# Two-layer pooling and HGRN2 trunk: one 128x128 product for a block's attention weights, and 32 bytes of padding among the activations

## The chip, the core and the metric

The kernel runs on one core of a Trainium2 chip. Its engines run side by side, each through its own list of instructions, and meet through semaphores: TensorE multiplies (PE in the profile; its weight loads are listed apart as PEld), VectorE (DVE) and ScalarE (ACT) read TensorE's results from PSUM and work in SBUF, GpSimd (POOL) works in SBUF, SyncE (SP) issues most transfers. The metric is the device time in microseconds (us), lower being better, as the median of several runs.

## What is computed

The input is 512 tokens of 1024 channels, float32. Layer 0 is a pooling mixer, layer 1 an HGRN2 mixer; each has a projection in, the mixer on 2048 inner channels, a gate, a projection out and a residual sum, and a final RMSNorm closes the trunk. The change lies in layer 1 (and in where the activations of both layers lie). For each of its 16 heads of 128 channels:

```python
log_f = logaddexp(log(lb), log1p(-lb) + log_sigmoid(fz))       # forget gate, per channel
k = (1 - lb) * sigmoid(-fz)
# o_t = S_t^T q_t  with  S_t = diag(f_t) S_{t-1} + k_t v_t^T
A[t, s] = sum_d q[t, d] * k[s, d] * exp(b[t, d] - b[s, d])      # s <= t, b = cumulative log_f
o = A @ v + (q * exp(b)) @ S
o = o * rsqrt(mean(o * o) + eps) * norm_g
y = (o * silu(gate)) @ w_out
```

## The kernel before

Activations lie channel-major ([channel, token]) in SBUF. The large projections multiply float32 numbers as three one-pass products of exact halves (`mm3`, L125 to L128: hi by hi, lo by hi, hi by lo), each with 128x128 weights loaded and 512 columns streamed past them. The streamed halves of the layer's input are xh0 to xh7 and xl0 to xl7 (`scaled_halves`, L197, in the pool `act`); those of the pooled values are ph and pl, of a mixer's result zh and zl (layer 0), z1h and z1l, and zz for the last group (layer 1, 256 columns a time). Weights arrive in pieces of 512 KB (`piece`, L97): SyncE issues the transfer into wraw, ScalarE casts the high half whi (L94), VectorE subtracts for wlo (L95).

Layer 1 goes through its heads in four groups of four (`group`, L425). For a group, `prepare` makes gates, keys and queries, `inputs` the values (here the pieces of the weights are streamed and slices of xh and xl are loaded as weights), and then `heads` (L576) does, on TensorE without large products between:

- `within` (L542) for each of the four heads: the weights of its four blocks of 128 tokens as plain float32 products, which TensorE runs in two passes each. A block takes two products that load 64 columns each: L549 (keys of the first half, 128 queries) into PSUM partitions 0 to 63, L550 (keys of the second half, only the 64 queries that can see them) into partitions 64 to 127. Then three transposes of the keys (L556). VectorE copies the causal part into Ad (L552, L553), ScalarE the transposed keys into kt (L558).
- `state` (L561) for each head: three products kt by vn (L567), which VectorE turns into the carried states st (L573, L574).

`attend` (L580) later multiplies Ad and the states with values and queries (L587, L589).

All these results go to the PSUM pool `pa` with four buffers. A product can only start when the buffer that it gets has been read: a head's transposes or weights wait for the copies of a head before it, and the second head's `state` product waits for the copy L553 of the third head. The large products have a pool `ps` of their own. The order on every engine is fixed when the program is built.

A second, general form of layer 1 (`levels`) lies behind a condition that is not met with these inputs; it doesn't run.

Of the kernel before, what the change touches and what calls it, by code (L numbers as in the profile page):

```python
"""Two-layer streaming-encoder trunk: multi-scale causal pooling mixer, then HGRN2, on one core.

Activations are kept channel-major ([channel, token]), so every projection contracts over
partitions.  float32 products with long moving operands run as three one-pass float32r products of
exact halves (x = hi + lo, 12 significant bits each): hi*hi + hi*lo + lo*hi.  Short ones run as
plain float32 products.

The RMSNorm factor of a token commutes with the projection, so it is applied where the projection's
result leaves PSUM.

HGRN2 is computed as causal linear attention.  The decay between tokens s < t is the product of the
forget gates of s+1..t.

Factored form: within a block of 128 tokens the decay is a ratio of products taken to the block's middle,
one factor going to k and one to q; from block to block the state is carried.  The products over half a
block must not run out of range for this; whether they did is recorded on the way.

General form, for any gates, run over the layer when the record says so: a pair is served at the one
level h (1, 2, 4, ..) at which s and t lie in sibling blocks of h tokens; the decay is then (s to the end
of its block) * (start of t's block to t), both at most one, so nothing can overflow.  The running products  # L20
are lengthened from level to level by the sibling's total.
"""
# [10 lines left out]
F32 = mybir.dt.float32  # L33
# [5 lines left out]
PSUM = bass.MemoryType.PSUM  # L39
# [5 lines left out]
KD = D // P          # 8 channel tiles of the model width  # L45
KI = DI // P         # 16 channel tiles of the inner width
NG = 4               # groups of the inner width
GC = DI // NG        # 512 channels a group
GT = GC // P         # 4 channel tiles a group
TB = T // P          # 4 token blocks  # L50
# [4 lines left out]
NORM_AT, SPREAD_AT = (KD - 2, 2), (KD - 1, 1)   # where in its first projection (step, tile)  # L55
AHEAD = 300           # how far, in traced instructions, the weights run ahead of their use
FLOOR = 1e-26         # the least product of gates over half a block that the factored form takes
LEVELS = (1, 2, 4, 8, 16, 32, 64)

# columns of the packed parameters  # L60
# [5 lines left out]
def trunk(ctx: ExitStack, tc: tile.TileContext, xT, par, ident_d, causal_d, mask_d, w0_in, w0_grp, w0_out, w1_in, w1_out, outT):  # L66
# [9 lines left out]
    # ---- parameters and constants  # L76
    ones = const.tile([P, P], F32, name="ones")
    nc.gpsimd.memset(ones, 1.0)
    # the tensor engine's clock comes up, and the function table in, while the first loads are on their way
# [17 lines left out]
    def piece(src):  # L97
        """A [128, 2, 512] piece of a weight as exact halves."""
        raw = wpool.tile([P, 2, GC], F32, name="wraw", tag="wraw", bufs=RAW)
        hi = wpool.tile([P, 2, GC], F32R, name="whi", tag="whi", bufs=WB)  # L100
        lo = wpool.tile([P, 2, GC], F32R, name="wlo", tag="wlo", bufs=WB)
        with tc.high_priority(AHEAD):
            nc.sync.dma_start(out=raw, in_=src)
            split(raw, hi, lo)
        return hi, lo

    def load_in(w, col=0):
        """512 columns of a projection: one pair of halves a row tile."""
        v = w.rearrange("(k p) n -> p k n", p=P)
        out = []  # L110
        for i in range(v.shape[1] // 2):
            hi, lo = piece(v[:, 2 * i:2 * i + 2, col:col + GC])
            out += [(hi[:, 0], lo[:, 0]), (hi[:, 1], lo[:, 1])]
        return out

    def load_out(w, g):
        """Rows of group g of a [2048, 1024] projection, one row tile a piece."""
        out = []
        for i in range(GT):
            r = g * GC + i * P  # L120
            hi, lo = piece(w[r:r + P, :].rearrange("p (a b) -> p a b", a=2))
            out.append((hi.rearrange("p a b -> p (a b)"), lo.rearrange("p a b -> p (a b)")))
        return out
# [6 lines left out]
    def project4(pieces, xs, norm):  # L130
        """The four channel tiles of 512 columns, advancing together through the contraction.  The norm's
        short products go in before the end, so that its result is there in time."""
        accs = [ps.tile([P, T], F32, name="mm", tag="mm", bufs=4) for _ in range(GT)]
        for k, ((wh, wl), (xh, xl)) in enumerate(zip(pieces, xs)):
            for n, acc in enumerate(accs):
                if (k, n) == NORM_AT:
                    rn = norm()
                if (k, n) == SPREAD_AT:
                    rb = spread_sbuf(rn)
                c = slice(n * P, (n + 1) * P)  # L140
                mm3(acc, wh[:, c], wl[:, c], xh, xl, k == 0, k == len(pieces) - 1)
        return accs, rn, rb

    def project(pieces, n, xs):
        """[128 channels, 512 tokens] of a projection: columns n*128.. of the pieces."""
        acc = ps.tile([P, T], F32, name="mm", tag="mm", bufs=4)
        c = slice(n * P, (n + 1) * P)
        for k, ((wh, wl), (xh, xl)) in enumerate(zip(pieces, xs)):
            mm3(acc, wh[:, c], wl[:, c], xh, xl, k == 0, k == len(pieces) - 1)
        return acc  # L150

    def rms(name, srcs, cols=slice(0, T)):
        """1/rms of each token over the channel tiles, [token, block]."""
# [29 lines left out]
    def spread(rn):  # L183
        """[token, block] -> [any channel, token], in PSUM."""
# [11 lines left out]

    def scaled_halves(k, col):  # L197
        g = pp[:, col + k:col + k + 1]
        hi = act.tile([P, T], F32R, name=f"xh{k}", tag=f"xh{k}", bufs=1)
        lo = act.tile([P, T], F32R, name=f"xl{k}", tag=f"xl{k}", bufs=1)  # L200
        nc.scalar.activation(out=hi, in_=h[k], func=AF.Copy, scale=g)
# [14 lines left out]
    # ---- layer 0: pooling mixer  # L216
# [83 lines left out]
    # kept for the general form of the next layer  # L300
# [4 lines left out]
    # ---- layer 1: HGRN2 mixer  # L305
    # lower bounds of this layer: softmax over the layers, cumulated, less the first
# [14 lines left out]
    def hgrn(ctx, general):  # L321
# [4 lines left out]
        # attention weights within a token block: zeroed once, later only the causal part is written  # L326
# [67 lines left out]
        def normed(o, so):  # L394
            """Each token of a head divided by its rms; so is left with the sums of squares."""
# [13 lines left out]
        def gated(g, n, on, gate, last):  # L409
            """Back to [channel, token], times the norm's weight and the gate."""  # L410
# [14 lines left out]
        def group(g, prepare, heads, zs):  # L425
            """One group of heads: the rest of its projections, its heads, and the output products of the
            group before, which keep the tensor engine busy meanwhile."""
# [19 lines left out]
        def finish(zs):  # L447
            """Last output product and final norm, one half of the tokens after the other."""
# [11 lines left out]
            def scaled(half, i, bc, rb):  # L460
                """Two channel tiles of the result; the first two by way of the engines that are free."""
# [27 lines left out]
        def factored():  # L489
            """Decays within a block of 128 tokens as ratios to its middle; between blocks by the state.  # L490
            Returns how many of the marks that say that the ratios stayed in range are set."""
# [9 lines left out]
            def store(f, pr, j, hd, s1):  # L501
                """In a block's first half at t the gate of t + 1 (one in the middle), in the second that of t."""
# [7 lines left out]
            def prepare(g):  # L510
# [3 lines left out]
                for pr in range(2):  # L514
# [6 lines left out]
                    # products over the halves, the first with the block's first gate as well  # L521
# [20 lines left out]
            def within(n):  # L542
                """Weights within the blocks; the tokens after the middle do not weigh on those before."""
# [3 lines left out]
                for b in range(TB):  # L547
                    c, m = b * P, b * P + 64
                    nc.tensor.matmul(a[0:64, b], k[:, c:m], q[:, c:c + P], start=True, stop=True)  # L549
                    nc.tensor.matmul(a[64:P, b, 64:P], k[:, m:c + P], q[:, m:c + P], start=True, stop=True)  # L550
# [10 lines left out]
            def state(g, n, kt, v):  # L561
                """The state that each block but the first starts from, taken on to the block's middle; by way
                of the block's start, as the two factors' product may be out of range."""
# [35 lines left out]
            # in range: no product over half a block under the floor, and every sum of squares finite  # L599
# [12 lines left out]
        def levels():  # L612
# [16 lines left out]
            def self_weights(pr, f, kk, q):  # L629
                """A token with itself: the decay is one.  Then q takes its own gate."""  # L630
# [8 lines left out]
            def level(pr, li, hh, tot, kk, q, off):  # L639
                """Pairs of sibling blocks of hh tokens; then the products are lengthened to 2 hh."""  # L640
# [90 lines left out]
def _masks():  # L731
    """For each level, which (s, t) of a token block lie in sibling blocks, for the t's in odd blocks."""
# [40 lines left out]
```

## Time and profile before

| what | value |
|---|---|
| device time, three runs | 845.63, 845.29, 845.55 us; median 845.55 us |
| span of the profiled execution, first to last instruction | 844.7 us |
| TensorE busy | 829.0 us, 98% of the span, 4134 passes |
| VectorE busy | 550.5 us, 65% |
| ScalarE busy | 274.6 us, 33% |
| GpSimd busy | 171.7 us, 20% |
| mean granted TensorE clock | 0.992 |
| HBM traffic | 92 GB/s over the span |

The profile's page gives the span of the profiled execution and no time of its own beside it; 845.55 less 844.7 leaves 0.85 us around the span. Starts are counted from the span's start. A matmul's duration in a row runs from its start to a modelled end, and the next one starts before that; the distance from start to start is what a product costs, and the texts below go by starts. A merged row (x24) stands for so many passes that follow one another.

### The profile page before, as it was taken

What the parts mean: (1) busy time and instruction counts of PE and PEld (TensorE: products, weight loads), DVE (VectorE), ACT (ScalarE), POOL (GpSimd) and SP (SyncE); (2) the same over time, 40 slices, a digit from 0 to 9 for tenths busy, and PEclk for the clock granted to TensorE, in tenths of its full rate; (3) what the DMA queues carried; (4) which work ended last, traced back from release to release, by engine and by line L of the source; (5) the groups of instructions that cost most, each with busy time, mean ns of one, the idle gap of its engine ahead of it and who ended that gap; (6) DMA issues with size and microseconds to landing.
All of it is one profiled execution on the core that took longest, in us unless ns stands there. A gap on an engine that the chain in (4) does not pass through costs nothing.

```text
span 844.7 us, 10684 instructions
## 1 busy us (share of the span) xinstructions
PE 829.0 (98%) x4134; PEld 691.7 (82%) x4134; DVE 550.5 (65%) x845; ACT 274.6 (33%) x472; POOL 171.7 (20%) x218
## 2 busy tenths in 40 slices
PE   9899999999999999999999999999999999999995
PEld 7688888888888888888888888888888888888895
DVE  7766645754685465799269963279963279963643
ACT  7352224213333144323332232332332332334231
POOL 5020001001002023170314300315300305203024
PEclk9999999999999999999999999999999999999997
DMA  6622333123423145133033331233331133320203
GB/s 217 209 70 84 99 100 100 55 96 100 150 99 100 54 163 180 57 95 105 1 100 100 100 100 30 71 100 100 99 101 39 62 100 100 100 100 1 74 2 104
DMA packets 37931, 78.56 MB, mean 93 GB/s; under 512 B 2800, under 2 KB 5104, under 8 KB 37872
## 3 DMA queue, kind: packets, MB, share of 16 engines
q1 hardware_dynamic: 35744, 74.98, 27.9%
q10 hardware_dynamic: 2128, 2.81, 0.9%
q8 instruction: 34, 0.56, 0.3%
q14 instruction: 25, 0.20, 0.1%
HBM read 73.59 MB, written 4.19 MB: 92 GB/s over the span
## 4 chain that ended last, share of the span: by engine, by line
PE 91%; DVE 4%; DMA 2%; POOL 1%; issue 1%; ACT 1%; SPq 0%; ACTq 0%; DVEq 0%; POOLq 0%
PE mm L126 28%; PE mm L128 27%; PE mm L127 27%; PE a L587 2%; DVE wlo L95 1%; PE a L549 1%; PE a L589 1%; PE a L567 1%; DVE r L534 1%; DMA wraw<-in_w0i 1%; PE a L414 1%; PE a L556 1%; DMA h<-in_xT 0%; DMA wraw<-in_w1i 0%; PE a L188 0%
## 5 line engine op out<-in xcount | busy, mean ns | idle before, releaser
L126 PE MATMUL mm<-xh,whi 128*128 128x512 f32 x640 | 251.3, 393 | 0.9 <-DVE v L242 0.4
L128 PE MATMUL mm<-xh,wlo 128*128 128x512 f32 x640 | 249.8, 391 | 1.6 <-DVE wlo L95 1.6
L127 PE MATMUL mm<-xl,whi 128*128 128x512 f32 x640 | 249.6, 390 | 0.0
L94 ACT CAST whi<-wraw 128x1024 fp32r<-128x1024 f32 (+1 forms) x140 | 141.8, 1025 | 249.8 <-PE mm L127 168.9
L95 DVE TENSOR_TENSOR wlo<-wraw,whi 128x1024 fp32r<-128x1024 f32 (+1 forms) x140 | 173.4, 1265 | 58.2 <-ACT whi L94 57.2
L128 PEld LDWEIGHTS mm<-xh,wlo 128*128 128x128 f32 x640 | 120.4, 188 | 28.6 <-DVE wlo L95 3.2
L126 PEld LDWEIGHTS mm<-xh,whi 128*128 128x128 f32 x640 | 120.6, 188 | 26.6 <-ACT whi L94 1.1
L127 PEld LDWEIGHTS mm<-xl,whi 128*128 128x128 f32 x640 | 120.5, 188 | 24.5
L214 DVE TENSOR_TENSOR h<-mm,h 128x512 f32<-128x512 f32 x56 | 38.5, 689 | 62.8 <-PE mm L128 62.5
L534 DVE RECIPROCAL r<-r 128x512 f32<-128x512 f32 x16 | 53.5, 3341 | 1.5 <-POOL r L533 1.5
L126 PE MATMUL mm<-zh,whi 128*128 128x512 f32 x128 | 50.4, 394 | 0.0
L128 PE MATMUL mm<-zh,wlo 128*128 128x512 f32 x128 | 50.2, 392 | 0.0
L126 PE MATMUL mm<-whi,xh 128*128 128x512 f32 x128 | 50.1, 391 | 0.0
L127 PE MATMUL mm<-wlo,xh 128*128 128x512 f32 x128 | 49.8, 389 | 0.0
L128 PE MATMUL mm<-whi,xl 128*128 128x512 f32 x128 | 49.8, 389 | 0.0
L127 PE MATMUL mm<-zl,whi 128*128 128x512 f32 x128 | 49.7, 388 | 0.0
L390 POOL TENSOR_TENSOR gs<-fz,s 128x512 f32<-128x512 f32 x16 | 20.7, 1293 | 98.6 <-ACT s L388 98.6
L272 POOL TENSOR_TENSOR gs<-gt,sg 128x512 f32<-128x512 f32 x16 | 21.2, 1328 | 91.7 <-ACT sg L270 91.5
L126 PE MATMUL mm<-z1h,whi 128*128 128x512 f32 x96 | 38.2, 398 | 0.0
L128 PE MATMUL mm<-z1h,wlo 128*128 128x512 f32 x96 | 38.0, 395 | 0.0
L127 PE MATMUL mm<-z1l,whi 128*128 128x512 f32 x96 | 38.0, 395 | 0.0
L402 POOL TENSOR_TENSOR ro<-mo,mhalf 128x4 f32<-128x4 f32 x16 | 16.2, 1015 | 104.0 <-DVE mo L400 104.0
(141 smaller groups left out, 1202.1 us busy)
## 6 DMA issues: line engine op xcount, KB each, us to landing
wraw<-in_w1i SPq DMA_DIRECT2D x64, 512.0 KB, 4.1
wraw<-in_w0i SPq DMA_DIRECT2D x28, 512.0 KB, 4.5
wraw<-in_w0o SPq DMA_DIRECT2D x16, 512.0 KB, 4.3
wraw<-in_w1o SPq DMA_DIRECT2D x16, 512.0 KB, 4.0
wraw<-in_w0g SPq DMA_DIRECT2D x8, 512.0 KB, 3.9
h<-in_xT SPq DMA_DIRECT2D x8, 256.0 KB, 5.1
wraw<-in_w0i SPq DMA_DIRECT2D x8, 256.0 KB, 5.0
hmid<-h ACTq DMA_DIRECT2D x8, 256.0 KB, 2.3
```

The costliest lines, as they stand in the source:

```text
L94: nc.scalar.copy(out=hi, in_=src)
L95: nc.vector.tensor_tensor(out=lo, in0=src, in1=hi, op=ALU.subtract)
L126: nc.tensor.matmul(out, lh, rh, start=start, stop=False)
L127: nc.tensor.matmul(out, lh, rl, start=False, stop=False)
L128: nc.tensor.matmul(out, ll, rh, start=False, stop=stop)
L214: nc.vector.tensor_tensor(out=h[n], in0=acc, in1=h[n], op=ALU.add)
L272: nc.gpsimd.tensor_tensor(out=gs, in0=gt, in1=sg, op=ALU.mult)
L390: nc.gpsimd.tensor_tensor(out=gs, in0=gt, in1=sg, op=ALU.mult)
L402: nc.gpsimd.tensor_tensor(out=ro[:, :, 0], in0=mo, in1=mhalf[:, :TB], op=ALU.pow)
L414: nc.tensor.transpose(out=oT[:, b * P:(b + 1) * P], in_=on[:, b], identity=ident)
L534: nc.vector.reciprocal(out=r, in_=r)
L587: nc.tensor.matmul(o[:, b], Ads[pr][:, j, t], v[:, b, n * P:(n + 1) * P], start=True, stop=b == 0)
```

## The change

A block's two products of 64 columns become one product with all 128 keys loaded and all 128 queries streamed; what it computes above the middle and below the diagonal is not copied by L552 and L553, which stay as they were (L557 and L558 after the change; lines behind the padding are five higher). And a tile of 32 bytes a partition is taken in the pool `act` once, behind xl3. The comments and docstrings are also left out.

```diff
+    padded = set()
+
     def scaled_halves(k, col):
         g = pp[:, col + k:col + k + 1]
         hi = act.tile([P, T], F32R, name=f"xh{k}", tag=f"xh{k}", bufs=1)
         lo = act.tile([P, T], F32R, name=f"xl{k}", tag=f"xl{k}", bufs=1)
+        if k == 3 and k not in padded:
+            padded.add(k)
+            act.tile([P, 8], F32, name=f"pad{k}")
...
             def within(n):
...
                 for b in range(TB):
-                    c, m = b * P, b * P + 64
-                    nc.tensor.matmul(a[0:64, b], k[:, c:m], q[:, c:c + P], start=True, stop=True)
-                    nc.tensor.matmul(a[64:P, b, 64:P], k[:, m:c + P], q[:, m:c + P], start=True, stop=True)
+                    t = slice(b * P, (b + 1) * P)
+                    nc.tensor.matmul(a[:, b], k[:, t], q[:, t], start=True, stop=True)
```

In the built program the padding moves every SBUF tile that is placed behind xl3 by 32 bytes: xh4 from byte 112928 of a partition to 112960, and likewise xl4 to xh7 and xl7, ph, zh, z1h, zz, kk, q, vn, Ad, kt and st. The weights' pieces (wraw, whi, wlo), xh0 to xh3 with their low halves, and the tiles h stay. Before, all the operands of the large products start 32 bytes behind a multiple of 64; after, the moved ones start at a multiple of 64.

TensorE's list is the only one in which instructions change; on the other four engines the same instructions stand in the same order. This is TensorE in the first group of layer 1, before, from the third head's transposes to the fourth head's weights (a is a buffer of `pa`, the operands are queries q, keys kk and the identity; in brackets the engines waited for):

```order
L556 MATMUL a<-ident,kk 128x128 [waits DVE_49]
L556 MATMUL a<-ident,kk 128x128 x2
L549 MATMUL a<-q,kk 64x128 [waits Activation_49]
L550 MATMUL a<-q,kk 64x64 [waits Pool_49]
L549 MATMUL a<-q,kk 64x128
L550 MATMUL a<-q,kk 64x64
```

And the same place after, with the fourth head's transposes:

```order
L561 MATMUL a<-ident,kk 128x128 [waits DVE_49]
L561 MATMUL a<-ident,kk 128x128 x2
L555 MATMUL a<-q,kk 128x128 [waits DVE_49,PE_49,Pool_49]
L555 MATMUL a<-q,kk 128x128 x3
L561 MATMUL a<-ident,kk 128x128 [waits Activation_49]
L561 MATMUL a<-ident,kk 128x128 x2
```

Eight products of a head (L549 and L550 by turns, four times) have become four, and two buffers of the pool have changed places: the fourth head's weights waited for ScalarE's copy of the second head's keys and now wait for VectorE's copy of the second head's weights; the fourth head's transposes waited for that one and now wait for ScalarE's. The four `state` products behind them wait for the same copies as before: ScalarE's of the third head, VectorE's of the third, ScalarE's of the fourth, VectorE's of the fourth.

## Rows read from the trace of the kernel before

**Rows 1.** The page: busy time by engine, and the chain that ended last.

```profile
PE 829.0 (98%) x4134; PEld 691.7 (82%) x4134; DVE 550.5 (65%) x845; ACT 274.6 (33%) x472; POOL 171.7 (20%) x218
...
PE 91%; DVE 4%; DMA 2%; POOL 1%; issue 1%; ACT 1%; SPq 0%; ACTq 0%; DVEq 0%; POOLq 0%
```

**Rows 2.** Waits of the weight loads: us in total, times, longest.

```profile
PEld a L549 <- issue: 3.1, 14, 0.4
PEld a L556 <- issue: 2.2, 13, 0.2
```

**Rows 3.** Timeline of TensorE, third group of heads: start us, us, line, operands, count.

```profile
619.21 0.39 PE L128 MATMUL mm<-whi,xl 128*128 128x512 f32 x1
619.53 0.32 PE L549 MATMUL a<-q,kk 128*64 128x128 f32 x1
...
620.54 0.55 PE L556 MATMUL a<-ident,kk 128*128 128x128 f32 x3
...
621.02 0.32 PE L549 MATMUL a<-q,kk 128*64 128x128 f32 x1
...
625.41 2.84 PE L567 MATMUL a<-vn,kt 128*128 128x128 f32 x24
```

**Rows 4.** Groups of TensorE by line and shape: busy us, mean ns.

```profile
L567 PE MATMUL a<-vn,kt 128*128 128x128 f32 x96 | 11.4, 275 | 0.0
```

**Rows 5.** Timeline of TensorE, transposes with large products on both sides.

```profile
426.10 1.03 PE L414 MATMUL a<-ident,on 128*128 128x128 f32 x8
426.89 0.48 PE L126 MATMUL mm<-xh,whi 128*128 128x512 f32 x1
```

**Rows 6.** Timeline of VectorE and ScalarE, first group of heads.

```profile
393.53 1.23 DVE L95 TENSOR_TENSOR wlo<-wraw,whi 128x1024 fp32r<-128x1024 f32 x1 [1.02 <-ACT whi L94]
...
395.00 0.43 DVE L553 COPY_PREDICATED Ad<-causal,a 128x256 f32<-128x256 uint8 x1
...
392.45 1.05 ACT L94 CAST whi<-wraw 128x1024 fp32r<-128x1024 f32 x1 [1.26 <-DMA wraw<-in_w1i]
```

**Rows 7.** Timeline of TensorE: the `state` products of the first, second and fourth group.

```profile
395.33 2.84 PE L567 MATMUL a<-vn,kt 128*128 128x128 f32 x24
...
499.25 2.84 PE L567 MATMUL a<-vn,kt 128*128 128x128 f32 x24
...
751.61 2.84 PE L567 MATMUL a<-vn,kt 128*128 128x128 f32 x24
```

**Rows 8.** Timeline of VectorE: the third head's last copy, second, third and fourth group.

```profile
498.92 0.43 DVE L553 COPY_PREDICATED Ad<-causal,a 128x256 f32<-128x256 uint8 x1
...
624.33 0.43 DVE L553 COPY_PREDICATED Ad<-causal,a 128x256 f32<-128x256 uint8 x1
...
750.79 0.42 DVE L553 COPY_PREDICATED Ad<-causal,a 128x256 f32<-128x256 uint8 x1
```

**Rows 9.** Timeline of TensorE: first and last of an unbroken run, streaming xh and xl.

```profile
72.12 0.39 PE L126 MATMUL mm<-xh,whi 128*128 128x512 f32 x1
...
75.97 0.39 PE L128 MATMUL mm<-xh,wlo 128*128 128x512 f32 x1
```

**Rows 10.** The same, streaming zh and zl, and then z1h and z1l.

```profile
109.71 0.39 PE L126 MATMUL mm<-zh,whi 128*128 128x512 f32 x1
...
112.92 0.39 PE L128 MATMUL mm<-zh,wlo 128*128 128x512 f32 x1
...
640.00 0.40 PE L126 MATMUL mm<-z1h,whi 128*128 128x512 f32 x1
...
642.80 0.40 PE L126 MATMUL mm<-z1h,whi 128*128 128x512 f32 x1
```

**Rows 11.** The same early in the run; then a stretch there: busy by engine, granted clock.

```profile
33.77 0.63 PE L127 MATMUL mm<-xl,whi 128*128 128x512 f32 x1
34.20 0.63 PE L128 MATMUL mm<-xh,wlo 128*128 128x512 f32 x1
...
33.54:35.68 2.14, 2.14 (x7) 1.66 (x6) 1.53 (x2) 1.52 (x2) 0.00 (x0) 0.50 0.45 172
```

## The prediction

> **What bounds the kernel now.** First the page's busy times and the chain that ended last: TensorE is busy for 98% of the span and carries 91% of the chain [rows 1]. So a time is won or lost only where TensorE's own list gets shorter, or where it begins to wait. Then the waits: between the large products it hardly waits for another engine, and what stands first for the small products of layer 1 is not an engine at all. The loads of L549 waited 3.1 us in 14 places and those of L556 2.2 us in 13, put down to "issue" [rows 2]. The timeline of one group of heads shows where these lie. In the third group the last large product starts at 619.21 and the first L549 at 619.53, 0.32 us later, where products of the same length follow each other after 0.2265 us (3.85 us for 17 steps, 72.12 to 75.97) [rows 3, 9]. A head then takes from 619.53 to 621.02, 1.49 us: 1.01 us for the weights of four blocks and 0.48 us for three transposes [rows 3]. Each time TensorE goes from large products to the 64-column ones, from these to the transposes, and back, some 0.09 us pass with nothing running.
>
> **The merged product, from the third group.** Now: 0.09 us at the entry, and 619.53 to 625.41 for four heads, 5.88 us, in all 5.97 us [rows 3]. After the change all of it runs with 128 columns loaded, like the `state` products. These take (2.84 - 0.275)/23 = 0.1115 us a pass [rows 3, 4], and I take this pace for the new product since it has the same shape, type and two passes: 4 blocks x 2 passes = 8 x 0.1115 = 0.89 us. A transpose between products of 128 columns takes (1.03 - 0.275)/7 = 0.108 us [rows 5], three 0.32 us. A head is 1.216 us, four are 4.86 us, and the group is 5.97 - 4.86 = 1.1 us shorter. The products themselves hardly save anything: L549 and L550 of a block ran side by side, so 8 steps of L549 with the switches filled the 1.01 us. What is saved is the switching, two of them a head.
>
> From both sides: were the new product's pass as slow as the pair with its switches, 1.01/8 = 0.126 us, only the transposes' switch would be left and a group would win 0.6 us; were it as quick as the transposes' 0.108 us, 1.2 us. The row of the same shape decides for 1.1.
>
> **What is late next.** A buffer of the pool must have been read before the next product starts, and VectorE and ScalarE don't get faster. The change brings no new wait on other engines; on TensorE the waits have changed places as the order shows. I followed each group with the copies as they stand in the trace. The tight one is the second head's `state` product, which waits for the third head's copy L553. It starts six passes, 0.67 us, behind the first of L567.
>
> - First group: 395.33 + 0.67 = 396.00 now [rows 7]. The copy runs from 395.00 to 395.43, behind a wlo of 1.23 us that started at 393.53 on a cast of ScalarE's, and that cast waited for its transfer until 392.45 [rows 6]. A faster TensorE doesn't pull any of these forward. So 0.57 us are won, not 1.1.
> - Second group: 499.25 + 0.67 = 499.92 now, the copy is done at 498.92 + 0.43 = 499.35 [rows 7, 8], behind a transfer again: 0.57 us.
> - Third: 625.41 - 1.1 + 0.67 = 624.98, and the copy is done at 624.76 [rows 3, 8]: the whole 1.1 us.
> - Fourth: 751.61 + 0.67 = 752.28 now, copy done at 751.21 [rows 7, 8]: 1.07 us.
>
> The fourth head's changed waits end earlier than these in the third and fourth group, and in the first two they lie ahead of the same copy. The sum is 0.57 + 0.57 + 1.1 + 1.07 = 3.3 us. Nothing gives it back later as far as the trace shows, since the large products behind each group start without a wait for weights or buffers and TensorE is full up to the tail.
>
> **The padding.** It adds no instruction. It can only matter by where the operands lie, and the trace has no run with an operand at a multiple of 64 bytes in the large products. But it has three groups of equal products at full clock that lie at different places, and they don't take the same time: xh and xl 0.2265 us a step [rows 9], zh and zl 3.21/14 = 0.229 us, z1h and z1l 2.80/12 = 0.233 us [rows 10]. So the place counts for up to 7 ns, 3%. I can't say from the rows which way 32 bytes go. Moved are: xh4 to xh7 and xl4 to xl7 as streamed operands, half of 1920 products, 960, and as loaded weights in half of `inputs`, 192; 576 products of ph, pl, zh and zl; 288 of z1; 192 short ones of zz.
>
> At the worst that the rows show, x and the loaded slices go to z1's pace: 1152 x 6.7 ns = 7.7 us lost. At the best that such rows show, the z's and z1 come down to x's pace: 576 x 2.5 ns + 288 x 6.7 ns = 1.4 + 1.9 = 3.3 us won. Further off lies the bare stream. In an early stretch where half the clock (1.2 GHz) was granted a step took 0.43 us, 33.77 to 34.20 [rows 11], which is one column a cycle; at 2.4 GHz 512 columns so take 0.213 us. Were all 1824 moved long streams to run at that, 960 x 13 + 576 x 16 + 288 x 20 ns = 27.5 us would be won. I take nothing: of the three places seen, x, which has 57% of what moves, is already at the best, and a shift may leave it, while z and z1 can gain; the two ends nearly balance.
>
> The Trainium skill, "TensorE: Matmul & The Clock Gate", section "Step-by-step: what each phase is for", says that TensorE reads streamed operand and weights through two separate ports, so that the next load takes nothing from the running product. By that rule the padding would be worth nothing, and the sum would stay at 3.3 us. The three paces above don't bear it out: equal products cost unequal time by what they stream.
>
> Profiled execution: 844.7 us of span and 0.85 us around it make the median of 845.55. Less 3.3 us: 841.4 us of span, **842.3 us**.
>
> **Rivals.**
>
> *The padding slows the moved streams a little* (0.18). If x's moved products and slices go to z's pace, 1152 x 2.5 ns = 2.9 us take back the gain: 845.2 us, no change. For it: x is at the lowest of three paces. Against it: all three kinds now start 32 bytes behind a multiple of 64 and still differ, so the step to a multiple of 64 does not by itself order them.
>
> *It slows them to z1's pace* (0.10). 7.7 - 3.3 = +4.4 us, 850.0 us, slower. It decides from 2.9 ns a product on (3.3 us / 1152), and over 0.2% from 4.3 ns.
>
> *It speeds up z and z1* (0.20). 3.3 us more: 839.0 us.
>
> *It frees the streams from the loads* (0.04). 842.3 - 27.5 = about 815 us. Against it: no product at full clock shows the bare pace.
> The same page's section "Back-to-back issue gap" gives 512/2.4 + 2.5, about 216 ns, as the gap at full clock; by it this rival would win an estimated 23 us instead, and no row here shows such a gap.
>
> *The merged product wins nothing* (0.05). If it had to wait for the copies at every head, the groups would keep their length and the time stays at 845.5 us. Against it: a head has two copies on VectorE, L553 taking 0.43 us [rows 8], and is still 1.2 us long.
>
> **How the numbers follow.** The forecast (0.43) is 842.3 us with 1.2 us on either side for the padding and the pass's pace, all of it faster by over 0.2% (1.7 us, about what a measurement of this kernel can tell from no change). With the two gains, faster has 0.43 + 0.20 + 0.04 = 0.67; same 0.18 + 0.05 = 0.23; slower 0.10. The range goes from 838.7 us (z and z1 sped up) to 846.8 us (the small loss with its spread); left out are the slow case and the freed streams, 0.14, and some of the edges.
>
> **What would show it.** TensorE's start-to-start for the new product: 0.11 us a pass, eight a head, and no "issue" rows of 0.17 us before L561. A head in the third group: 1.22 us. The second `state` product of the first two groups should start right behind the third head's copy. For the padding: the steps of xh4 to xh7 against those of xh0 to xh3, which didn't move, and of zh and z1h against 0.229 and 0.233 us. If xh4's step differs from xh0's by over 2 ns, the forecast is wrong by the padding; if the third group isn't 1.1 us shorter, by the product.

## The result and the profile after

The changed kernel takes 852.67 us (median of 4 runs, 852.16 to 853.97) where the kernel before, on the same chip, takes 845.59 us (845.29 to 847.14): a ratio of 1.0081, 95% interval 1.0069 to 1.0094. It is slower by 7 us; the prediction said 842.3 us, and its range ended at 846.8 us.

The page of the changed kernel, busy time by engine and the chain that ended last:

```profile
PE 833.4 (98%) x4006; PEld 690.9 (81%) x4006; DVE 550.2 (65%) x845; ACT 274.0 (32%) x472; POOL 170.4 (20%) x218
...
PE 94%; DMA 2%; DVE 1%; ACT 1%; issue 1%; POOL 1%; ACTq 0%; DVEq 0%; POOLq 0%
```

TensorE has 128 passes less than in [rows 1], 4006 for 4134, and is busy for 4.4 us longer. The other engines do what they did. So the time was not lost in a wait: the same products took longer.

The timeline of TensorE shows which. First the third group of heads, start us, us, line, operands, count, as in [rows 3] (the lines lie five further down: L555 the merged product, L561 the transposes, L572 the `state` products):

```profile
624.69 0.40 PE L128 MATMUL mm<-whi,xl 128*128 128x512 f32 x1
624.92 1.05 PE L555 MATMUL a<-q,kk 128*128 128x128 f32 x8
625.81 0.49 PE L561 MATMUL a<-ident,kk 128*128 128x128 f32 x3
626.14 1.06 PE L555 MATMUL a<-q,kk 128*128 128x128 f32 x8
...
629.80 2.84 PE L572 MATMUL a<-vn,kt 128*128 128x128 f32 x24
```

A head takes 626.14 - 624.92 = 1.22 us where it took 1.49 us, and the first one starts 0.23 us behind the last large product, without the 0.09 us of an entry. The group as a whole is 1.1 us shorter. The merged product did what it was to do.

Now one tile of queries, an unbroken run of 24 products, xh0 to xh7 with three products each. The rows are its first product (xh0), the first with xh4, and the first product of the next tile. Behind them are the first and the last of the runs with zh and zl and with z1h that [rows 10] show of before:

```profile
235.97 0.40 PE L126 MATMUL mm<-xh,whi 128*128 128x512 f32 x1
...
238.73 0.40 PE L126 MATMUL mm<-xh,whi 128*128 128x512 f32 x1
...
241.53 0.40 PE L126 MATMUL mm<-xh,whi 128*128 128x512 f32 x1
...
109.18 0.40 PE L126 MATMUL mm<-zh,whi 128*128 128x512 f32 x1
...
112.44 0.39 PE L128 MATMUL mm<-zh,wlo 128*128 128x512 f32 x1
...
644.37 0.40 PE L126 MATMUL mm<-z1h,whi 128*128 128x512 f32 x1
...
647.17 0.40 PE L126 MATMUL mm<-z1h,whi 128*128 128x512 f32 x1
```

Before, 12 such products took 2.72 us, whichever x they streamed (0.2265 us a step in [rows 9]), but for a first tile behind other products, of which the section on the hardware speaks. Now the 12 with xh0 to xh3, tiles that didn't move, take 2.76 us (230 ns a step), and the 12 with xh4 to xh7, which moved by 32 bytes, 2.80 us (233 ns). A run with zh and zl takes 3.26 / 14 = 233 ns a step where it took 229, and z1h 2.80 / 12 = 233 ns as before. Each tile of 24 products loses 0.12 us, and there are 80 of them.

### The profile page after: what moved, and what is told of

Read it like the earlier page. It is cut to its first block, busy times and chain, and to the rows that moved or that the text cites. A ratio compares the mean times of both kernels' runs of the same rounds, so it can differ in the third digit from the quotient of the medians.

```text
span 850.4 us, 10438 instructions
## 1 busy us (share of the span) xinstructions
PE 833.4 (98%) x4006; PEld 690.9 (81%) x4006; DVE 550.2 (65%) x845; ACT 274.0 (32%) x472; POOL 170.4 (20%) x218
## 4 chain that ended last, share of the span: by engine, by line
PE 94%; DMA 2%; DVE 1%; ACT 1%; issue 1%; POOL 1%; ACTq 0%; DVEq 0%; POOLq 0%
PE mm L126 29%; PE mm L128 29%; PE mm L127 28%; PE a L592 2%; PE a L555 2%; PE a L572 1%; PE a L594 1%; DMA wraw<-in_w0i 1%; PE a L419 1%; PE a L561 1%; DMA wraw<-in_w0g 1%; ACT whi L94 0%; DMA pp<-in_par 0%; DVE wlo L95 0%; PE a L173 0%
## 5 line engine op out<-in xcount | busy, mean ns | idle before, releaser
L126 PE MATMUL mm<-xh,whi 128*128 128x512 f32 x640 | 254.3, 397 | 1.7 <-DVE v L247 1.1
L128 PE MATMUL mm<-xh,wlo 128*128 128x512 f32 x640 | 251.8, 394 | 0.4 <-DVE wlo L95 0.3
L127 PE MATMUL mm<-xl,whi 128*128 128x512 f32 x640 | 250.7, 392 | 0.0
L128 PEld LDWEIGHTS mm<-xh,wlo 128*128 128x128 f32 x640 | 120.0, 188 | 30.5 <-DVE wlo L95 1.3
L126 PEld LDWEIGHTS mm<-xh,whi 128*128 128x128 f32 x640 | 120.2, 188 | 28.7 <-DVE v L247 1.6
L127 PEld LDWEIGHTS mm<-xl,whi 128*128 128x128 f32 x640 | 120.1, 188 | 27.2
L126 PE MATMUL mm<-zh,whi 128*128 128x512 f32 x128 | 51.1, 399 | 0.0
L126 PE MATMUL mm<-whi,xh 128*128 128x512 f32 x128 | 50.5, 395 | 0.0
L128 PE MATMUL mm<-zh,wlo 128*128 128x512 f32 x128 | 50.4, 394 | 0.0
L128 PE MATMUL mm<-whi,xl 128*128 128x512 f32 x128 | 50.4, 394 | 0.0
L127 PE MATMUL mm<-zl,whi 128*128 128x512 f32 x128 | 50.2, 392 | 0.0
L127 PE MATMUL mm<-wlo,xh 128*128 128x512 f32 x128 | 50.2, 392 | 0.0
L126 PE MATMUL mm<-z1h,whi 128*128 128x512 f32 x96 | 38.2, 398 | 0.0
L128 PE MATMUL mm<-z1h,wlo 128*128 128x512 f32 x96 | 38.0, 396 | 0.0
L127 PE MATMUL mm<-z1l,whi 128*128 128x512 f32 x96 | 38.0, 395 | 0.0
```

The costliest lines, as they stand in the source:

```text
L126: nc.tensor.matmul(out, lh, rh, start=start, stop=False)
L127: nc.tensor.matmul(out, lh, rl, start=False, stop=False)
L128: nc.tensor.matmul(out, ll, rh, start=False, stop=stop)
```

## Experiments

The theory after the look at the two traces was that the padding did it, by the place of the streamed tile, and that the merged product alone would win what it was thought to win. The rival was that the new product, with its other order of PSUM buffers, had disturbed the streams itself. All kernels below were timed against the kernel before, in 3 rounds.

In the built programs the places of the tiles can be read. Before, whi, wlo and all x's start at 32 bytes past a multiple of 256, ph, pl, zh and zl at 96, z1h and z1l at 224. As the paddings below move whole pieces of this layout, "distance" here means the start of the streamed tile less that of the loaded weights' tile, within 256 bytes: before it is 0 for x, 64 for p and z, 192 for z1. After the change it is 0 for xh0 to xl3, 32 for xh4 to xl7, 96 for p and z, 224 for z1.

**The merged product alone.** From the changed kernel:

```diff
-        if k == 3 and k not in padded:
-            padded.add(k)
-            act.tile([P, 8], F32, name=f"pad{k}")
```

> The changed kernel without its padding: one product of 128 columns a block, every tile where it lay before. If the padding did the harm (padding theory), the groups' heads are short by 1.0 to 1.3 us each, 4.4 us in all, the streams step as before (226 to 228 ns for every xh and xl, p and z 229, z1 233), and the time is about 841 us. If the merged product itself, by its other order of PSUM buffers or by another draw of the clock, slowed the streams (schedule theory), xh4 to xh7 step at 231 to 236 ns here too and the time is about 852 us.

Measured: 841.6 us, ratio 0.9958 (0.9942 to 0.9975). All streams step as before: x at 227 ns, p and z at 229, z1 at 233. The rows are the first product with xh4 and the first of the next tile, 2.72 us apart:

```profile
235.16 0.39 PE L126 MATMUL mm<-xh,whi 128*128 128x512 f32 x1
...
237.88 0.39 PE L126 MATMUL mm<-xh,whi 128*128 128x512 f32 x1
```

The new product is what it seemed to be, and the schedule theory falls.

**The padding alone.** The kernel before with those three lines added.

> The kernel before with the 32 bytes of padding alone, the products of 64 columns kept. Padding theory: heads as before, xh4 to xh7 step at 231 to 236 ns, xh0 to xh2 a little slower than 227, p and z 233 instead of 229: about 12 us more, 857 us. Schedule theory: as before, 845.5 us.

Measured: 857.35 us, ratio 1.0144 (1.0127 to 1.0161). The same tile of queries as above in this kernel's timeline:

```profile
238.03 0.40 PE L126 MATMUL mm<-xh,whi 128*128 128x512 f32 x1
...
240.79 0.40 PE L126 MATMUL mm<-xh,whi 128*128 128x512 f32 x1
...
243.59 0.40 PE L126 MATMUL mm<-xh,whi 128*128 128x512 f32 x1
```

2.76 and 2.80 us again, without the merged product. So 32 bytes that nobody reads or writes cost 12 us here (857.35 less 844.89 for the kernel before in these rounds), and some 10.4 us in the changed kernel: it lost 7.1 us where the merged product alone won 3.3 us, each against the kernel before of its own rounds.

**Everything moved together.** The merged product, no padding between the x's, but 32 bytes in front of the weights:

```diff
     act = ctx.enter_context(tc.tile_pool(name="act", bufs=1))
+    wpool.tile([P, 8], F32, name="wpad")
```

> The merged product, with 32 bytes put in front of all activations and behind nothing that TensorE loads or streams apart: the weights' halves, xh0 to xl7 and everything behind them all move by 32 bytes together, so that the distance from any loaded weight to any streamed tile is what it was before, but every tile stands on another place of its own. If the distance between the loaded and the streamed operand counts (distance theory), the streams step as before, 227 ns, and the time is that of the merged product alone, about 841 us. If the streamed tile's own place counts (own-place theory: a start at a multiple of 64 bytes is slower), all eight x's, not four, step at about 233 ns, and the time is near 860 us.

Measured: 841.67 us, ratio 0.9965 (0.9951 to 0.9979). Every x now starts at a multiple of 64 bytes, as xh4 to xh7 do in the changed kernel, and the same tile (one line further down) takes 2.72 and 2.72 us:

```profile
232.92 0.39 PE L127 MATMUL mm<-xh,whi 128*128 128x512 f32 x1
...
235.64 0.39 PE L127 MATMUL mm<-xh,whi 128*128 128x512 f32 x1
...
238.36 0.39 PE L127 MATMUL mm<-xh,whi 128*128 128x512 f32 x1
```

A tile's own place, changed by these 32 bytes, doesn't count. What counts is where it lies against the others.

**256 bytes in the place of 32.** The changed kernel with `act.tile([P, 64], ...)`.

> The changed kernel with 256 bytes of padding in the place of 32; to make room the scratch tile that takes the squares of the head norm has one buffer instead of two, which only ScalarE writes and nobody reads. xh4 to xl7 and all behind lie 256 bytes further than before. If what counts repeats with 256 bytes or a divisor of it (32 apart), the steps are those of before and the time is about 841 us. If any gap in the row of tiles costs, xh4 to xh7 step at 231 to 236 ns and the time is about 852 us.

Measured: 841.88 us, ratio 0.9963 (0.9949 to 0.9977). The rows are the first product with xh4 and the first of the next tile, 2.72 us apart:

```profile
235.62 0.39 PE L126 MATMUL mm<-xh,whi 128*128 128x512 f32 x1
...
238.34 0.39 PE L126 MATMUL mm<-xh,whi 128*128 128x512 f32 x1
```

A gap in the row of tiles costs nothing when it is 256 bytes.

**All x's 32 bytes from the weights.** The merged product with the padding in front of xh0 instead of behind xl3:

```diff
     small = ctx.enter_context(tc.tile_pool(name="small", bufs=2))
+    act.tile([P, 8], F32, name="front")
```

> The merged product, with 32 bytes between the weights' halves and xh0: all eight x's and everything behind them lie 32 bytes further from the weights than in the merged product alone; among themselves the x's lie as before. If the distance from the loaded to the streamed operand counts, all of xh0 to xl7 step at about 233.5 ns instead of 227: some 1900 streams by 6.6 ns are 12.5 us, p and z at 233 add 2.5 us, and the projections that load the x's 2.8 us, so about 859 us. If instead the break in the row of tiles between xl3 and xh4 cost, the x's step at 227 ns here, and only p and z are slower: about 844 us.

Measured: 856.97 us, ratio 1.0132 (1.0113 to 1.0152). The same tile:

```profile
237.73 0.40 PE L127 MATMUL mm<-xh,whi 128*128 128x512 f32 x1
...
240.53 0.40 PE L127 MATMUL mm<-xh,whi 128*128 128x512 f32 x1
...
243.33 0.40 PE L127 MATMUL mm<-xh,whi 128*128 128x512 f32 x1
```

2.80 and 2.80 us: all eight x's are slow, though they lie among themselves as before. The distance to the weights decides, not a break between the tiles. Of the 2 us less than expected, 0.9 us are the first group's wait for a copy (see below), which is gone here.

**64 and 128 bytes.** The changed kernel with `act.tile([P, 16], ...)` and with `act.tile([P, 32], ...)`.

> The changed kernel with 64 bytes of padding in the place of 32 (the scratch tile of the head norm's squares has one buffer instead of two, for the room). xh4 to xl7 lie 64 bytes from the weights' place within 256, p and z 128, z1 at 0. Distance theory, with the pace that each distance had before: xh4 to xl7 at 229 ns as p and z had at 64 (950 streams by 2.3 ns, 2.2 us more), z1 at 227 instead of 233.3 (288 streams, 1.9 us less), p and z at 128 unknown, between 227 and 233 ns: 841 to 844 us. If the distance does not count by itself, but any that is not a multiple of 256 costs the same, xh4 to xl7 are at 233.5 and the time is about 848 us.

> The same with 128 bytes of padding. xh4 to xl7 lie 128 bytes from the weights' place within 256, p and z 192, z1 64. Distance theory: p and z at 233.3 as z1 had at 192 (576 streams by 3.5 ns, 2 us more), z1 at about 229 (1.2 us less), xh4 to xl7 at 128 unknown: 842 us if 128 is as good as 0, 851 us if it is as bad as 32, the xh0 to xh2 behind them included.

Measured: 848.9 us (ratio 1.0036, 1.0019 to 1.0053) and 849.93 us (1.0059, 1.0039 to 1.0078). With 64 bytes first the tile of queries (first product with xh0, with xh4, with xh5, and the next tile), then the ends of the z1h run, whose tiles the padding happened to bring to distance 0:

```profile
236.18 0.40 PE L126 MATMUL mm<-xh,whi 128*128 128x512 f32 x1
...
238.95 0.40 PE L126 MATMUL mm<-xh,whi 128*128 128x512 f32 x1
...
239.66 0.39 PE L126 MATMUL mm<-xh,whi 128*128 128x512 f32 x1
...
241.72 0.40 PE L126 MATMUL mm<-xh,whi 128*128 128x512 f32 x1
...
642.56 0.39 PE L126 MATMUL mm<-z1h,whi 128*128 128x512 f32 x1
...
645.28 0.39 PE L126 MATMUL mm<-z1h,whi 128*128 128x512 f32 x1
```

z1h came down from 2.80 to 2.72 us for its 12 steps, as the distance theory has it. The time missed the 841 to 844 us of the expectation, and the x's take 2.77 and 2.77 us, 231 ns a step, the unmoved xh0 to xh3 as slow as the moved ones. Product by product the moved ones differ: from xh5 to the end of the tile a step takes 2.06 / 9 = 229 ns, what z had at 64, but xh4, the first tile behind the change of distance, takes 0.71 / 3 = 236 ns here and 234 on average over the tiles. With 128 bytes (same tile):

```profile
235.49 0.39 PE L126 MATMUL mm<-xh,whi 128*128 128x512 f32 x1
...
238.23 0.40 PE L126 MATMUL mm<-xh,whi 128*128 128x512 f32 x1
...
241.02 0.39 PE L126 MATMUL mm<-xh,whi 128*128 128x512 f32 x1
```

2.74 and 2.79 us. By the starts of all tiles xh4 to xh7 step at 232 to 235 ns here, xh0 at 232 and xh1 to xh3 at 227; z1, now at 64, steps at 229 ns, and p and z, now at 192, at 233, the paces that z and z1 had at these distances before. So of the distances tried only 0 (256) is free, and a run that stays at one distance has the pace of that distance: 229 ns at 64, some 232 at 128, 233 at 32, 96, 192 and 224. What looking up the pace left out is the passage from one distance to another, which x makes twice a tile: the tiles behind it, unmoved ones too, take up to some 6 ns more a step than the pace of their own distance.

**Only wlo moved.** The merged product; 32 bytes between whi and wlo, and 224 in front of xh0, so that all but wlo keeps its place within 256 bytes:

```diff
+            if i == 0:
+                wpool.tile([P, 8], F32, name="wpad")
             lo = wpool.tile([P, 2, GC], F32R, name="wlo", tag="wlo", bufs=WB)
...
     small = ctx.enter_context(tc.tile_pool(name="small", bufs=2))
+    act.tile([P, 56], F32, name="front")
```

> The merged product without the padding of the change; 32 bytes between whi and wlo, and 224 bytes in front of xh0, so that only wlo stands 32 bytes off: whi, all x's, p, z and z1 keep their places within 256 bytes (the scratch tile of the squares has one buffer, for the room). The three products of a tile stream xh, xl, xh and load whi, whi, wlo. If the running stream and the load for the product behind it disturb each other, the step that grows is that of L127, in which xl streams while wlo is loaded: from 226.6 to 231 to 236 ns, with L126 as before and L128 as before but for what carries over. If it is the pair within one product, the step of L128 grows (wlo its weight, xh its stream) and L127 stays. A third of the streams by 6.6 ns is some 4 us, less what z and z1 make of it: about 846 us. If the load of the weights has no part in it at all, and it is the streamed tiles' order among themselves: 841.6 us.

Measured: 856.02 us, ratio 1.0118 (1.0094 to 1.0142). Three products of one tile (L127, L128, L129 here; in the text on record L126, L127, L128), with the weight load of the third, and the tile's end:

```profile
237.56 0.40 PE L127 MATMUL mm<-xh,whi 128*128 128x512 f32 x1
237.79 0.40 PE L128 MATMUL mm<-xl,whi 128*128 128x512 f32 x1
238.03 0.39 PE L129 MATMUL mm<-xh,wlo 128*128 128x512 f32 x1
...
237.79 0.19 PEld L129 LDWEIGHTS mm<-xh,wlo 128*128 128x128 f32 x1
...
243.16 0.40 PE L127 MATMUL mm<-xh,whi 128*128 128x512 f32 x1
```

No streamed x changed its place within 256 bytes, only a weight that is loaded for one product in three, and the tile takes 5.60 us as with all x's moved. So the load has its part in it. By the starts of all tiles the three steps take 232, 239 and 228 ns: the one in which xl streams while wlo is loaded for the next product (both start at 237.79) grew most, by some 13 ns, as the pairing of the running stream with the next load would have it. The product that has wlo as its own weight grew least, by 2 ns, so the pair within one product is not what counts most; but the first one grew by 5 ns too, with its operands and the load beside it in their old places. p and z went from 229 to 231 ns, z1 from 233 to 231. The 4 us of the expectation counted the one step alone and missed the rest.

**p, z and z1 to the weights' place.** The merged product, with 192 bytes in front of p's tiles (z's move along) and 64 in front of z1's:

```diff
+    pads = {'p': 48, 'z1': 16}
+
     def halves(src, tag, bufs, pool=act):
+        if tag in pads:
+            pool.tile([P, pads.pop(tag)], F32, name=f"pad{tag}")
```

> The merged product without the padding of the change, and with paddings of another kind: 192 bytes in front of the tiles of p (those of z move with them) and 64 in front of those of z1, so that p, z and z1 all lie at the weights' own place within 256 bytes, as the x's do. Distance theory: p and z step at 227 instead of 229 (576 streams, 1.4 us less), z1 at 227 instead of 233.3 (288 streams, 1.9 us less), all else as in the merged product alone: 838.3 us, less than either kernel. If the pace of z and z1 has another reason (the waits around them, the function of the engines beside), nothing changes: 841.6 us.

Measured: 838.7 us, ratio 0.9927 (0.9904 to 0.995): faster than either kernel, by 7 us than before and, by the two ratios, by 13 us than the change. The runs of z and z1 again:

```profile
107.93 0.39 PE L126 MATMUL mm<-zh,whi 128*128 128x512 f32 x1
...
111.11 0.39 PE L128 MATMUL mm<-zh,wlo 128*128 128x512 f32 x1
...
633.21 0.39 PE L126 MATMUL mm<-z1h,whi 128*128 128x512 f32 x1
...
635.93 0.39 PE L126 MATMUL mm<-z1h,whi 128*128 128x512 f32 x1
```

3.18 / 14 = 227 ns for z, 2.72 / 12 = 227 ns for z1. The three paces that the prediction found in the trace of before were three distances, and with the distances gone they are one pace.

**The small products too.** The same with kk, q, Ad, vn, kt and st at the weights' place, by paddings of 64, 192 and 192 bytes; the scratch tile of the squares has one buffer here too.

> The version with p, z and z1 at the weights' place, and the same done for the small float32 products of the heads by paddings of 64 bytes in front of the attention weights Ad, 192 in front of kk and 192 in front of q (128 in front of z1 to keep its place): kk, q, Ad, vn, kt, st and both zz tiles now all lie at 32 within 256 bytes. If a product of 128 columns loses to the distance as the ones of 512 do, a pass of the merged product goes from 0.111 us towards the transposes' 0.108, and the time, with some 450 such passes by up to 5 ns, towards 836.5 us. If the short ones are bound by something else, 838.5 us as without these paddings.

Measured: 838.49 us, ratio 0.9904 (0.9883 to 0.9925), the same as without. Eight passes of the merged product take 0.89 us, as in the changed kernel:

```profile
386.37 1.05 PE L560 MATMUL a<-q,kk 128*128 128x128 f32 x8
387.26 0.49 PE L566 MATMUL a<-ident,kk 128*128 128x128 f32 x3
```

The merged product's two operands stood 64 bytes apart without these paddings and 0 with them; over the whole trace it takes 111.5 ns a pass either way, and so do the products of Ad and vn, which were 128 apart. These float32 products of 128 columns don't see the distance.

## Why the prediction was wrong

**What bounds the kernel** was read rightly: TensorE's own list sets the time, and a step of a few nanoseconds more counts in full, since some 3000 large products run one behind another.

**The merged product** was right. A head takes 1.22 us and the "issue" rows are gone, as predicted. Two switches a head are worth 0.27 us (1.49 less 1.22), some 0.13 us each and not the 0.09 us that the text gives each; the sum did not suffer, since it was taken from whole heads. Alone the product made 844.89 us into 841.6, the predicted 3.3 us. By the starts in the traces, from the last large product ahead of a group to the first behind it, in us:

```text
group                  1      2      3      4     sum
before               9.14   8.86   8.80   8.81   35.61
merged product       8.61   7.71   7.71   7.71   31.74
padding alone        8.81   8.81   8.81   8.81   35.24
changed kernel       7.71   7.71   7.71   7.71   30.84
```

The heads won 3.9 us by this table, 0.6 us more than predicted. The interval of the run is 2.1 to 4.9 us, so it can't tell the two apart, and that the median met the 3.3 us is partly luck.

In the first group the wait came as predicted: 0.53 us were won instead of 1.1, and the trace of the merged product alone names it. TensorE (first two rows) waits behind six passes for VectorE's copy of the third head (third row):

```profile
392.45 0.93 PE L567 MATMUL a<-vn,kt 128*128 128x128 f32 x6
393.62 2.27 PE L567 MATMUL a<-vn,kt 128*128 128x128 f32 x18 [0.24 <-DVE Ad L553]
...
393.14 0.42 DVE L553 COPY_PREDICATED Ad<-causal,a 128x256 f32<-128x256 uint8 x1
```

In the second group it did not: 1.15 us were won where 0.57 were given. The step took the end of the copy, behind a transfer, as given. First the second group's first head, the issue of the transfers (SPq) and the cast behind the first of them in the kernel before, then the three in the kernel with the merged product:

```profile
493.30 0.32 PE L549 MATMUL a<-q,kk 128*64 128x128 f32 x1
...
491.71 7.36 SPq L103 DMA_DIRECT2D wraw<-in_w1i  x4
...
496.37 1.05 ACT L94 CAST whi<-wraw 128x1024 fp32r<-128x1024 f32 x1 [0.99 <-DMA wraw<-in_w1i]
```

```profile
490.90 1.05 PE L550 MATMUL a<-q,kk 128*128 128x128 f32 x8
...
489.40 6.59 SPq L103 DMA_DIRECT2D wraw<-in_w1i  x4
...
493.29 1.04 ACT L94 CAST whi<-wraw 128x1024 fp32r<-128x1024 f32 x1 [0.50 <-DMA wraw<-in_w1i]
```

The transfer is issued at the same place, 1.59 and 1.50 us ahead of the head, but from its issue to the cast it took 4.66 us before and 3.89 us with the merged product. In the second group of all ten kernels with the merged product it takes 3.7 to 3.9 us, and 4.6 us with the padding alone. So the 0.57 us rested on a slow transfer that did not come again with the merged product; why it is slow there in both kernels with the old products is not shown. In the changed kernel no group waits at all. Its streams, slower by 0.12 us a tile, bring TensorE to the heads late enough for the copies to be done, and the padding alone took the first group's old wait away in the same way. So 4.8 us were won in the heads of the changed kernel, 0.4 of them by the padding itself, and the loss in the streams was larger than the 7 us of the result: with the 12.5 us that the padding alone cost and the 4.4 us (35.24 less 30.84) that the product wins beside it, the parts give 845.6 + 12.5 - 4.4 = 853.7 us, where 852.67 was measured.

**The padding** is the step that failed: "I take nothing". It cost 10.4 to 12.5 us, and the worst end that was given, 7.7 us, was too small as well. By the steps it is made up of the 960 moved streams of x at 233.3 instead of 226.7 ns (6.3 us); 960 streams of x that did not move, at 230 (3 us); 576 of p and z at 233 instead of 229 (2.4 us); and the projections that load the moved x's (192 by some 6 ns, 1.1 us). That is 12.8 us, of which the waits that went away in the heads give back 0.4 us without the merged product (35.61 less 35.24) and 0.9 us with it (31.74 less 30.84). The bound left out the second and third item: it took it that only a moved operand can be slower, and that p and z could only gain.

The rows held more than was read out of them. Three kinds of products with three paces, all starting 32 bytes past a multiple of 64, were taken to balance gains and losses; the forecast then rested on a mean of two ends. But the one kind at the best pace was also the one whose tiles stood, within 256 bytes, exactly where the weights stood, and the text looked at the streamed tile's place alone. Had it set each pace beside its distance (0: 226.5 ns; 64: 229; 192: 233), the padding, which takes half of x from distance 0 and puts nothing else on it, had a loss to offer for x, and no row gave p, z and z1 a better pace at their new distances, 96 and 224. The rival "it slows them to z1's pace" (850.0 us, 0.10) had the right sign and, for the moved x's, the right pace; by the distances it deserved more than 0.10.

By the Trainium skill, "TensorE: Matmul & The Clock Gate", section "Step-by-step: what each phase is for", the load of the next weights takes no read bandwidth from the running product. No run here bears that out for tiles at another place than the weights': moving wlo alone, an operand that is only loaded in these products, made the streams of x slower by 6.6 ns on average.

## What to carry to other kernels

Where TensorE is full with products of 512 columns and a weight load for each, as here, look at the places of the loaded and the streamed tiles before counting on anything of a few per cent: equal products that differ in pace are a hint that is in the trace already, and bringing all operands to the same place within 256 bytes was worth some 3 us here (841.6 and 838.7 us, from different rounds; the steps of p, z and z1 in the two traces give 3.1 us), without an instruction. A change that adds or takes a tile whose bytes a partition are no multiple of 256 in front of them moves everything behind it, and its effect should be timed apart from what it came with. And a saving may look larger than it is when something else in the same change slows the kernel down around it: the heads won 3.9 us alone, 4.8 us beside the padding.

## What the hardware did that was not expected

**Distance.** Three large products in a row (xh, xl, xh with whi, whi, wlo) take 680 ns when all operands stand at the same place within 256 bytes, and 700 ns when the x's are 32 bytes off, or when only wlo is. Not even the best pace, 226.7 ns, is the 216 ns that the Trainium skill, "TensorE: Matmul & The Clock Gate", section "Back-to-back issue gap", gives for the isolated gap of a product at full clock, worked out as 512 / 2.4 + 2.5; no run here came near it.

**It carries over.** Products whose operands did not move are slower behind products whose did. The same is in the kernel before, where xh0 to xh3 follow a run of p (first product with xh0, first with xh4), beside the version with p at distance 0:

```profile
223.26 0.40 PE L126 MATMUL mm<-xh,whi 128*128 128x512 f32 x1
...
226.03 0.39 PE L126 MATMUL mm<-xh,whi 128*128 128x512 f32 x1
```

```profile
220.81 0.39 PE L126 MATMUL mm<-xh,whi 128*128 128x512 f32 x1
...
223.53 0.39 PE L126 MATMUL mm<-xh,whi 128*128 128x512 f32 x1
```

2.77 us against 2.72. In the changed kernel, where each tile but the first follows xl7 at distance 32, xh0 and xh1 take 232 ns a step by the starts of all tiles, xh2 228, and xh3 is back at 227.

**What stays open** is why. The runs show that the load takes part, that moving all by the same 32 bytes changes nothing, that 256 bytes are as good as none, and that something outlasts a product; they don't show where in the chip two reads meet. Whether a stream without any load beside it would run at the same pace from every place was not tried.
